# A hybrid decoder trunk on one core: three more warm-up matmuls, halved first loads on two queues, and other PSUM banks for the forget-gate turns

## The chip, the core and the metric

The kernel runs on one core of one Trainium2 chip. Everything is float32 data. The metric is the device time of the whole program in microseconds, the median of several executions; lower is better.

The engines are called as in the profile: PE is TensorE's matmul side and PEld its weight loads, DVE is VectorE, ACT is ScalarE, POOL is GpSimd, SP is SyncE. SP computes nothing here: it issues DMAs. ACT and POOL issue a few of them as well.

## The reference, cut to what matters

Two layers over a sequence of 256 tokens with 2048 features. Layer 0 mixes with two parallel recurrent groups, layer 1 with dilated attention; each layer ends in a squared-ReLU MLP with 8192 hidden features. What the change touches lies in layer 0, in its norm, its input projection and the HGRN2 group:

```python
hn = rms_norm(h, norm_mix[0])
proj = hn @ w_in                        # 2048 -> 6144 columns
x_lru, y_lru, q_h, f_h, v_h, g_h = split(proj)
# HGRN2, 8 heads of width 128, chunkwise
q = silu(q_h)
log_f = log(lower_bound + (1 - lower_bound) * sigmoid(f_h))
k = (1 - lower_bound) * sigmoid(-f_h)
# per chunk: decayed products of q and k, applied to v, and a carried state
...
h = h + concat(lru, hgrn) @ w_out
h = h + square(relu(rms_norm(h, norm_mlp[0]) @ w1)) @ w2
```

## The kernel before, in words

**Matmuls.** A float32 operand is held as two parts, `hi` (the value cast to a shorter float32 form) and `lo` (the rest). A product takes three matmuls, hi·hi, hi·lo and lo·hi; below, such a group is called a triple. ACT makes `hi` by a cast and DVE makes `lo` by a subtraction, for each weight tile of 128x2048 and for the activations (`bufa`, `bufb`). The matmuls are issued through `mm`, which chains each to the one before: PE's order is that of the code. All of them carry line 241 in the profile, and the turns (transposes on PE through the identity `ident`) line 244. All operations of DVE and ACT carry line 68, the helper that can keep an engine in written order. Outside that helper's ordered part, which begins after the first projection group, a scheduler with its own model of times decides the order on DVE, ACT and SP.

**The opening.** Line 301 issues WARM = 9 matmuls of 128x128 on a tile of ones; their result is not used. Each is two records in the profile (x18 for nine). Then `fetch_first` (line 206) loads the first inputs. The tensor `head` holds, for each of the first 8 slabs of 128 features, the tokens' values (256 columns) beside the first weight columns (512). Slabs 0 to 3 come as four pieces of 384 KB, slabs 4-5 and 6-7 as two of 768 KB (line 213), then `x_in` with the other slabs and the weight tiles `raw` (lines 221, 224). All are issued by SP; the small table `cols` (gains, biases) is issued by ACT (line 303). For each slab ACT scales the tokens (`bufa`, hi) and casts the weights (`hi`), and DVE makes the two lo parts. The first projection group, v0, is computed slab by slab (`by_k`): for each slab two triples, one for each half of the tokens, accumulated in two PSUM tiles `p`.

**Counters of DMAs.** Each DMA that SP or ACT issues reports its landing on one of eight counters, given out in turn in the order of the program. Before a counter is used again, the issuing engine waits until its last DMA has landed. So at most eight such DMAs are under way, and the ninth issue waits for the first landing.

**The groups of layer 0.** The projection is computed in groups of 512 columns in the order `v0 x0 x1 q0 G0 f0 q1 f1 G1 v1 g0 y0 g1 y1` (G0 and G1 are the gates of the LRU). Between halves of weight tiles, `tick` advances other work by one step, by the table TICKS. Lanes a and b each run `hgrn` for a pair of heads, hgrn(0) and hgrn(1) first, later hgrn(2) and hgrn(3). The first steps of one `hgrn`: turn q into a PSUM bank, take its sigmoid (ACT) and scale by it (DVE); turn f, take two sigmoids of it (ACT); then products of k and q in a bank of its own, and the levels c = 1, 2, 4 ... 128, each with matmuls into a tile named "pl". PSUM tiles: "pd" and "pt" have one bank each (lane a uses "pd", lane b "pt"), "pl" has two banks, which the LRU gates and the levels share, "p" has three, "po" one. A turn into a bank waits until the readers of its last contents are done.

Of the kernel before, what the change touches and what calls it, by code (L numbers as in the profile page):

```python
# [10 lines left out]
F32 = mybir.dt.float32  # L11
# [9 lines left out]
P = 128  # L21
S = 256
# [19 lines left out]
def trunk_kernel(ctx, tc, head, x, xtok, cols, tab, masks, pos, fin, w_in, w_gate, w_out, w_qkv, w_o, w1, w2, out):  # L42
    nc = tc.nc
# [9 lines left out]
    psc = pool("psc", 1, space=PSUM)  # L53
# [45 lines left out]
    both_in = opening.tile([P, 8, S + 512], F32, name="both_in")  # L99
# [32 lines left out]
    at = [0, 0]  # L132
# [73 lines left out]
    def fetch_first():  # L206
        for u in range(4):
            at[0] += 1
            if u < 2:
                made[u] = Weights(None, 0)  # L210
                m = u + 1
                for k in range(4 * u, 4 * u + 4, m):
                    nc.sync.dma_start(both_in[:, k:k + m], head[:, k:k + m])
                    for i in range(k, k + m):
                        split_to(bufa[:, i], both_in[:, i, :S], col("nmix0", i))
                        made[u].split((i - 4 * u) * 512, 512, both_in[:, i:i + 1, S:])
                continue
            r = wraw.tile([P, 2048], F32, name="raw")
            src, i = units[u]
            made[u] = Weights(r, 0)  # L220
            nc.sync.dma_start(x_in[:, 4 * u - 8:4 * u - 4], x[:, 4 * u - 8:4 * u - 4])
            n = 1024 if u == 2 else 2048
            for m in range(0, 2048, n):
                nc.sync.dma_start(r[:, m:m + n], src[i][:, m:m + n])
            for m in range(2):
                for k in range(4 * u + 2 * m, 4 * u + 2 * m + 2):
                    split_to(bufa[:, k], x_in[:, k - 8], col("nmix0", k))
                made[u].split(1024 * m, 1024)
# [14 lines left out]
    def turn(out_, in_):  # L243
        chain[:] = [after(T.transpose(out_, in_, ident), chain)]  # L244
# [26 lines left out]
    def lut(out_, in_, func, **kw):  # L271
        i = A.activation(out_, in_, func, **kw)
        if luts["kind"] != tables[func]:
            luts.update(kind=tables[func], before=luts["now"], now=[])
        luts["now"].append(after(i, luts["now"][:1] or luts["before"]))
# [8 lines left out]
    def split_to(dst, src, gain=None):  # L284
        if gain is None:
            h, l = dst[..., :S], dst[..., S:]
            A.copy(h, src)
            V.tensor_tensor(l, src, h.bitcast(F32), OP.subtract)
        else:
            A.activation(dst[:, :S], src, AF.Copy, scale=gain)  # L290
            V.scalar_tensor_tensor(dst[:, S:], src, gain, dst[:, :S].bitcast(F32),
                                   op0=OP.mult, op1=OP.subtract)
# [6 lines left out]
    warm = psc.tile([P, P], F32, name="po", bufs=1)  # L299
    for _ in range(WARM):  # L300
        T.matmul(warm, ones, ones, start=True, stop=True)
    with tc.high_priority():
        nc.scalar.dma_start(c_, cols)
        fetch_first()
# [92 lines left out]
    m = tmp.tile([P, 2], F32, name="nm2", bufs=2)  # L397
# [93 lines left out]
    done = {"v0": vfirst}  # L491
    outs, roots, rooms = {}, {}, {}

    def turned(name, tiles, at):
        p = psc.tile([P, 2, S], F32, name=name, bufs=1)
        for i, (z, m) in enumerate(zip(tiles, at)):
            for j in range(2):
                turn(p[:, i, j * P:j * P + P], z[:, j, m * P:m * P + P])
        return p
# [4 lines left out]
    def hgrn(c2):  # L504
        g, at = c2 // 2, 2 * (c2 % 2)
        bank = "pt" if at else "pd"
# [4 lines left out]
        f = xall[:, slot + 1024:slot + 1536].rearrange("p (h s) -> p h s", h=2)  # L511
        rest = [slot + 1536]
        p = turned(bank, [done[f"q{g}"]] * 2, (at, at + 1))
        lut(qp, p, AF.Sigmoid)
        for h, hd in enumerate(heads):
            V.scalar_tensor_tensor(qp[:, h], p[:, h], omlb[:, hd:hd + 1], qp[:, h], op0=OP.mult, op1=OP.mult)
        yield
        p = turned(bank, [done[f"f{g}"]] * 2, (at, at + 1))
        lut(f, p, AF.Sigmoid)
        lut(kq, p, AF.Sigmoid, scale=-1.0)  # L520
        for h, hd in enumerate(heads):
# [13 lines left out]
        while c <= 128:  # L535
            yield
            pl = psc.tile([P, 2, 2, 64], F32, name="pl", bufs=2)
# [60 lines left out]
    def finish(g, half):  # L598
        if not half:
            hs = roots[g]  # L600
            V.tensor_scalar(hs, hs, 1.0 / P, EPS, op0=OP.mult, op1=OP.add)
            roots[g] = wk.tile([P, 8], F32, name="hr", bufs=2)
            rsqrt(roots[g], hs, 8)
            yield
        pair_ = [2 * half, 2 * half + 1]
        for at in pair_:
            o, z = outs[4 * g + at], done[f"g{g}"][:, :, at * P:at * P + P]
            s = wk.tile([P, 2, P], F32, name="g", bufs=2)
            lut(s, z, AF.Sigmoid)
            V.tensor_tensor(s, s, z, OP.mult)  # L610
            for j in range(2):
                V.scalar_tensor_tensor(o[:, j], o[:, j], roots[g][:, 2 * at + j:2 * at + j + 1], s[:, j],
                                       op0=OP.mult, op1=OP.mult)
        yield
        p = turned("po", [outs[4 * g + at] for at in pair_], (0, 0))
        if g and not half:
            bufb.tiles[3] = act.tile([P, 4, 2 * S], F32R, name="bufb3")
        for i, at in enumerate(pair_):
            split_to(bufb[:, 8 + 4 * g + at], p[:, i], col("gn", 4 * g + at))
        yield  # L620
# [66 lines left out]
    def reload():  # L687
        for j in range(2):
            nc.sync.dma_start(xres[:, j], xtok[:, j])

    lanes.update(a=[hgrn(0), hgrn(2)], b=[hgrn(1), hgrn(3)],
                 c=[lru_in(0, 0), lru_in(0, 1), lru_in(1, 0), lru_in(1, 1),
                    lru_gelu(0), lru_out(0, 0), lru_out(0, 1), lru_gelu(1), lru_out(1, 0), lru_out(1, 1)],
# [421 lines left out]
    for g in range(4):  # L1115
        z = columns(8 + 8 * g, "qk", 2, True)
        todo = [steps.pop(0) if steps else [] for _ in range(14)]
        for i in range(4):
            turned, scores, weights, mixed = attend(4 * g + i, z)
# [18 lines left out]
    done = [n for n in range(4) if n != LAST]  # L1138
    rr = []
    with urgent():  # L1140
        for j in range(2):
            m = tmp.tile([P, 1], F32, name="fm", bufs=2)
# [15 lines left out]
        for j in range(2):  # L1158
            for n, e in ((0, A), (1, V), (3, A), (LAST, V)):
                at = slice(n * 512, n * 512 + 512)  # L1160
# [7 lines left out]
            for h in range(2):  # L1168
                at = slice(h * 1024, h * 1024 + 1024)
# [21 lines left out]
}  # L1191
PLACE = {step: n for n, step in enumerate(step for step in ORDER.split() if step[0] != "G")}
WARM = 9
ONES = 240
PLACES = ((2, 3, 5, 6), (2, 5, 8, 9), (3, 7, 10, 11), (4, 9, 12, 13))
LINE = 64
# [98 lines left out]
```

## Time and profile before

| | |
|---|---|
| median of 3 runs | 2128.49 us (2128.37, 2128.49, 2129.51) |
| the profiled execution | 2129.77 us, of which its span 2128.0 us |
| PE busy | 2116.4 us (99% of the span), 9822 matmul records |
| PEld, DVE, ACT busy | 1763.7, 1779.9, 1310.7 us |
| POOL busy | 72.3 us |
| HBM read, written | 496.41 MB, 2.10 MB (234 GB/s over the span) |

The profile is of one execution. Its times are counted from the start of the span. A row of the timeline has start, duration (both us), engine, line, operation, output <- inputs, count, and in brackets the idle time of the engine just before it and what ended that. The ends of matmuls are modelled, and neighbouring matmuls overlap. Queues are marked by a q: SPq is SP issuing a DMA, and a row there tells of the issue, not of the transfer.

### The profile page before, as it was taken

To read this page: it belongs to the slowest core of one execution; us is meant where nothing else is said; L and a number is where in the kernel's file an instruction comes from. 1 tells how busy PE (TensorE), PEld (TensorE's weight loads), DVE (VectorE), ACT (ScalarE), POOL (GpSimd) and SP (SyncE) were. 2 spreads that over 40 slices of the span, in tenths; PEclk is the share of its full clock that TensorE was granted. 3 is DMA by queue.
4 is the path that set the end of the run, shared out by engine and by line. 5 is a ranking of instruction groups with operands and counts; after the bars stand their busy time and mean duration, and the time that the engine had idled before them with its cause. 6 is when DMAs were issued, how large, how long until landed. Compare 5 with 4: busy or idle time off the path is not lost.

```text
span 2128.0 us, 24856 instructions
## 1 busy us (share of the span) xinstructions
PE 2116.4 (99%) x9822; PEld 1763.7 (83%) x9822; DVE 1779.9 (84%) x1687; ACT 1310.7 (62%) x1325; POOL 72.3 (3%) x89
## 2 busy tenths in 40 slices
PE   9999999999999999999999999999999999999998
PEld 8888888888888888888888888888888888888887
DVE  6666768988888888888998888798988987988897
ACT  7556466666566566566665666566755655755664
POOL 0000000000000000000000000000000000000000
PEclk9999999999999999999999999999999999999999
DMA  8543456787878778787778667567788778787874
GB/s 336 187 158 141 165 190 217 227 264 242 254 240 271 249 247 249 266 254 227 241 266 257 218 204 224 205 217 241 235 249 280 234 243 270 244 256 238 275 260 157
DMA packets 70164, 500.12 MB, mean 235 GB/s; under 512 B 7840, under 2 KB 8096, under 8 KB 10272
## 3 DMA queue, kind: packets, MB, share of 16 engines
q1 hardware_dynamic: 57888, 412.99, 50.7%
q0 software_dynamic: 11872, 84.94, 21.2%
q8 instruction: 77, 1.26, 0.2%
q10 hardware_dynamic: 288, 0.61, 0.1%
q14 instruction: 39, 0.32, 0.0%
HBM read 496.41 MB, written 2.10 MB: 234 GB/s over the span
## 4 chain that ended last, share of the span: by engine, by line
PE 96%; DVE 2%; ACT 1%; issue 0%; DMA 0%; DVEq 0%; ACTq 0%
PE p L241 60%; PE pd L241 15%; PE po L241 14%; PE pt L241 3%; PE pl L244 2%; PE pl L241 2%; DVE lo L68 1%; ACT hi L68 1%; ACT bufb L68 0%; ACT tk L68 0%; DVE xc L68 0%; DMA both_in<-in_head 0%; DVE tk L68 0%; DVE bufb L68 0%; DVE xall L68 0%
## 5 line engine op out<-in xcount | busy, mean ns | idle before, releaser
L68 DVE TENSOR_TENSOR lo<-raw,hi 128x2048 fp32r<-128x2048 f32 (+1 forms) x364 | 788.7, 2171 | 236.3 <-ACT hi L68 235.1
L68 ACT CAST hi<-raw 128x2048 fp32r<-128x2048 f32 (+1 forms) x364 | 659.3, 1817 | 497.6 <-PE p L241 306.8
L241 PE MATMUL p<-hi,bufa 128*128 128x512 f32 x2000 | 644.7, 393 | 0.6 <-ACT bufa L68 0.6
L241 PEld LDWEIGHTS p<-hi,bufa 128*128 128x128 f32 x2000 | 376.4, 188 | 78.3 <-ACT bufa L68 0.9
L241 PE MATMUL p<-hi,bufb 128*128 128x512 f32 x1264 | 404.9, 390 | 0.0
L241 PE MATMUL p<-lo,bufa 128*128 128x512 f32 x1000 | 389.9, 390 | 0.0
L68 DVE TENSOR_TENSOR lo<-s,hi 128x2048 fp32r<-128x2048 f32 x120 | 274.1, 2284 | 11.4 <-ACT hi L68 9.4
L241 PEld LDWEIGHTS p<-hi,bufb 128*128 128x128 f32 x1264 | 237.3, 188 | 49.0
L68 ACT CAST hi<-s 128x2048 fp32r<-128x2048 f32 x120 | 229.6, 1913 | 51.4 <-PE po L241 22.6
L241 PE MATMUL p<-lo,bufb 128*128 128x512 f32 x632 | 245.9, 389 | 0.0
L241 PEld LDWEIGHTS p<-lo,bufa 128*128 128x128 f32 x1000 | 188.4, 188 | 37.7
L241 PEld LDWEIGHTS p<-lo,bufb 128*128 128x128 f32 x632 | 118.7, 188 | 24.2
L241 PE MATMUL pd<-hi,bufa 128*128 128x512 f32 x352 | 116.7, 393 | 0.0
L241 PE MATMUL p<-hi,formx 128*128 128x512 f32 x352 | 116.2, 391 | 0.0
L68 DVE TENSOR_TENSOR lo<-t,hi 128x2048 fp32r<-128x2048 f32 x40 | 91.5, 2287 | 15.9 <-ACT hi L68 15.9
L241 PE MATMUL po<-hi,bufb 128*128 128x512 f32 (+1 forms) x320 | 102.3, 386 | 0.0
L241 PE MATMUL p<-hi,formh 128*128 128x512 f32 x288 | 94.5, 389 | 0.0
L68 DVE TENSOR_TENSOR s<-s,raw 128x2048 f32<-128x2048 f32 x40 | 91.2, 2281 | 0.6 <-DMA raw<-in_w_qkv 0.6
L68 DVE TENSOR_TENSOR s<-raw,t 128x2048 f32<-128x2048 f32 x40 | 91.3, 2283 | 0.2 <-DMA raw<-in_w_o 0.2
L68 ACT ACTIVATE y<-y 128x512 f32<-128x512 f32 x112 | 68.8, 630 | 28.1 <-DVE y L68 27.3
L241 PE MATMUL po<-hi,bufa 128*128 128x512 f32 x256 | 84.9, 393 | 0.0
L68 ACT CAST hi<-t 128x2048 fp32r<-128x2048 f32 x40 | 76.5, 1914 | 12.3 <-PE po L241 6.3
(293 smaller groups left out, 2786.9 us busy)
## 6 DMA issues: line engine op xcount, KB each, us to landing
raw<-in_w SPq DMA_DIRECT2D x224, 1024.0 KB, 6.5
raw<-in_w_in SPq DMA_DIRECT2D x45, 1024.0 KB, 4.8
raw<-in_w_qkv SPq DMA_DIRECT2D x42, 1024.0 KB, 6.5
t<-in_w SPq DMA_DIRECT2D x32, 1024.0 KB, 6.5
t<-in_w POOLq DMA_DIRECT2D x32, 1024.0 KB, 8.6
s<-in_w POOLq DMA_DIRECT2D x32, 1024.0 KB, 8.8
raw<-in_w_out SPq DMA_DIRECT2D x15, 1024.0 KB, 4.8
raw<-in_w_o SPq DMA_DIRECT2D x15, 1024.0 KB, 4.8
```

Of the source, the lines that this page charges most:

```text
L68: i = call(*args, **kw)
L241: chain[:] = [after(T.matmul(*args, **kw), chain)]
L244: chain[:] = [after(T.transpose(out_, in_, ident), chain)]
```

## The change

Three edits. WARM goes from 9 to 12. Each of the four pieces for slabs 0 to 3 is loaded as two DMAs of 64 partitions, the lower half issued by SP and the upper half by ACT; the pieces of slabs 4-5 and 6-7 stay whole and on SP. The turns of the forget gates f go into a "pl" bank (of which there are two) in place of the bank of the lane, "pd" or "pt", that holds q.

```diff
@@ fetch_first
                 for k in range(4 * u, 4 * u + 4, m):
-                    nc.sync.dma_start(both_in[:, k:k + m], head[:, k:k + m])
+                    for half, queue in enumerate((nc.sync, nc.sync if u else nc.scalar)[:1 if u else 2]):
+                        ps_ = slice(0, P) if u else slice(64 * half, 64 * half + 64)
+                        queue.dma_start(both_in[ps_, k:k + m], head[ps_, k:k + m])
                     for i in range(k, k + m):
@@ turned
-        p = psc.tile([P, 2, S], F32, name=name, bufs=1)
+        p = psc.tile([P, 2, S], F32, name=name, bufs=2 if name == "pl" else 1)
@@ hgrn
-        p = turned(bank, [done[f"f{g}"]] * 2, (at, at + 1))
+        p = turned("pl", [done[f"f{g}"]] * 2, (at, at + 1))
         lut(f, p, AF.Sigmoid)
@@
-WARM = 9
+WARM = 12
```

## The prediction

> **What bounds the kernel now.** I read the page first, for the share of TensorE.
>
> ```profile
> span 2128.0 us, 24856 instructions
> ## 1 busy us (share of the span) xinstructions
> PE 2116.4 (99%) x9822; PEld 1763.7 (83%) x9822; DVE 1779.9 (84%) x1687; ACT 1310.7 (62%) x1325; POOL 72.3 (3%) x89
> ```
>
> PE is busy for 2116.4 of 2128.0 us, so only 11.6 us can be saved by taking waits away. Next I asked for the list of waits on PE alone, over the whole span.
>
> ```profile
> PE pd L244 <- DVE xall L68: 1.4, 1, 1.4
> PE po L301 <- DVE e L68: 1.1, 1, 1.1
> PE p L241 <- ACT bufa L68: 0.6, 1, 0.6
> PE pt L244 <- DVE xall L68: 0.2, 1, 0.2
> ```
>
> Columns: total us, times, longest. Four waits, 3.3 us in all: the start (1.1), the gap between warm-up and first real matmul (0.6), and one pair of turns that waits for its banks (1.4 and 0.2). The busy time of each engine by stretch says whether anything else gives way.
>
> ```profile
> 20.00:100.00 80.00, 80.00 (x375) 66.80 (x374) 56.18 (x112) 49.01 (x51) 0.70 (x1) 1.00 0.66 246
> 132.00:320.00 188.00, 188.00 (x1016) 161.89 (x1015) 124.82 (x200) 102.51 (x172) 0.00 (x0) 1.00 0.45 164
> 320.00:2119.00 1799.00, 1798.81 (x8207) 1493.54 (x8207) 1560.13 (x1312) 1115.81 (x1032) 71.36 (x84) 1.00 0.76 242
> ```
>
> The second and third columns are the stretch and PE's busy time: the same number, but for 0.2 us. So whatever PE gains or loses before 20 us, or around 129 us, arrives at the end undiminished, and nothing else pays. The other 11.6 - 3.3 = 8.3 us lie behind the last matmul and are not touched.
>
> The order in which the changed program was built agrees with this reading: PE's sequence is the old one with three warm-up matmuls more and other bank names at the eight forget-gate turns of each group. On VectorE and ScalarE it differs in the first 15 us, in some small operations after v0, and by a few neighbours swapped near 350 us. PE was not idle in either place (rows above), so these go at nothing, with PE's own matmuls as their cover; without it each would cost one small operation, under 1 us. So there are two terms.
>
> **Term 1, the forget gates.** In `hgrn` the f turn now takes a "pl" bank, where it took the bank that the q turn of the same lane had filled.
>
> ```profile
> 125.31 0.69 ACT L68 ACTIVATE tk<-p,nr 128x512 f32<-128x512 f32 x1 [0.33 <-PE p L241]
> ```
> ```profile
> 129.17 0.86 DVE L68 SCALAR_TENSOR_TENSOR xall<-pt,omlb,xall 128x256 f32<-128x256 f32 x2
> ```
> ```profile
> 129.39 0.63 PE L244 MATMUL pd<-tab__183,tk 128*128 128x128 f32 x4 [1.40 <-DVE xall L68]
> 130.18 0.63 PE L244 MATMUL pt<-tab__183,tk 128*128 128x128 f32 x4 [0.16 <-DVE xall L68]
> ```
>
> PE stood 1.40 and then 0.16 us until VectorE had read q out of "pd" and "pt" (the second read is the middle row). The data of f0 were there from about 126.0 (125.31 + 0.69, upper row). Is a "pl" bank free then? Here are its last reader before and its next writer after:
>
> ```profile
> 102.83 0.87 ACT L68 ACTIVATE bufb<-pl,c__91 128x256 f32<-128x256 f32 x2
> ```
> ```profile
> 143.37 1.89 PE L241 MATMUL pl<-xall 128*128 128x64 f32 x16
> ```
>
> It ended at 103.7, 24 us earlier; the next user of "pl", the first level, is the second row, 14 us later. So 1.56 us go, once: the same turns of the second group, near 219 us, have no entry in the list of waits. What is late next? After the turn PE goes on with the second half of a weight tile whose first half it has just used, so nothing new is awaited. Term 1: **-1.56 us**, between 0 and -1.6.
>
> **Term 2, the opening.** Here is who starts what before.
>
> ```profile
> 0.74 3.07 SPq L213 DMA_DIRECT2D both_in<-in_head  x6
> 0.74 0.40 ACTq L303 DMA_DIRECT2D c__91<-in_cols  x1
> ...
> 1.05 4.21 PE L301 MATMUL po<-nr 128*128 128x128 f32 x18 [1.05 <-DVE e L68]
> ...
> 4.98 0.88 SPq L224 DMA_DIRECT2D raw<-in_w_in  x2
> ...
> 5.90 0.79 PE L241 MATMUL p<-hi,bufa 128*128 128x512 f32 x1 [0.63 <-ACT bufa L68]
> ...
> 10.31 0.33 SPq L396 DMA_DIRECT2D xall<-in_xtok  x1
> 10.31 0.51 ACT L68 ACTIVATE bufa<-both_in,c__91 128x256 fp32r<-128x256 f32 x1 [0.81 <-DMA both_in<-in_head]
> ```
>
> Nine warm-ups take 4.21 us, so twelve take 5.61 and end at 6.66: 0.76 us after the first real matmul started before. By itself that is a loss. It is paid back if the matmul rate doubles sooner:
>
> ```profile
> 5.90:9.47 3.57, 3.57 (x8) 2.83 (x9) 3.24 (x7) 2.91 (x6) 0.00 (x0) 1.00 1.00 358
> 9.47:13.40 3.93, 3.93 (x18) 3.25 (x17) 3.25 (x8) 3.12 (x8) 0.00 (x0) 1.00 1.02 420
> ```
>
> Eight matmuls in 3.57 us (0.45 each), then eighteen in 3.93 (0.22 each): the slow rate cost 8 x 0.23 = 1.8 us here, although the column of the granted clock says 1.00 in both. That is the most a better warm-up could bring.
>
> But I think neither sets the start any more; the order of the loads does. Eight counters serve the DMAs of SP and ACT in turn, and a ninth DMA waits until the holder of its counter has landed. Before, six pieces and x_in were issued without such a wait, and the ninth DMA (row 4.98) waited for `cols`. With eight halves in place of four pieces, the piece of slabs 4 and 5 is now the ninth: SP holds it until `cols` has landed, at 4.98 instead of about 2.8 (the fifth of six in 3.07 us from 0.74). Behind it on SP stand piece 6-7, x_in and the first weight tiles, each held by the counter of a half that is early; POOL's queue is not passed. And the second half of slab 3 stands on ACT's queue behind slab 1's casts. The scheduler has accordingly put slabs 4 and 5 **ahead of slab 3** on ACT and DVE, while PE still takes slab 3 first. So PE now waits for three slabs' work that begins when piece 4-5 lands (call that T).
>
> T: bytes moved in the stretches of before,
>
> ```profile
> 0.00:4.98 4.98, 3.93 (x18) 3.92 (x18) 0.19 (x3) 1.65 (x3) 0.20 (x4) 1.00 0.64 190
> 4.98:6.97 1.99, 1.36 (x5) 0.91 (x4) 1.50 (x4) 1.82 (x4) 0.00 (x0) 1.00 0.96 324
> 6.97:8.48 1.51, 1.51 (x5) 1.22 (x4) 1.48 (x3) 1.02 (x2) 0.00 (x0) 1.00 1.01 372
> 8.48:10.31 1.83, 1.83 (x7) 1.41 (x7) 1.42 (x3) 1.01 (x2) 0.00 (x0) 1.00 1.01 420
> ```
>
> (last column GB/s) are 946, 645, 562 and 769 KB, 2922 in all when piece 4-5 landed at 10.3. The late half of slab 3 (197 KB) now comes behind it, which is worth 0.47 us at 420 GB/s: T = 9.8. The lower end is the issue at 4.98 plus the fastest landing of such a piece,
>
> ```profile
> DMA to landing us min/median/max: 4.1/5.8/8.8
> ```
>
> 4.98 + 4.1 = 9.1; the upper end is the old 10.3. I take 9.7, near the row of bytes. Three slabs from there, as before from the row 10.31:
>
> ```profile
> 12.04 0.39 PE L241 MATMUL p<-lo,bufa 128*128 128x512 f32 x1
> ...
> 13.37 0.68 DVE L68 TENSOR_TENSOR lo<-both_in,hi 128x512 fp32r<-128x512 f32 x1
> 13.40 0.39 PE L241 MATMUL p<-lo,bufa 128*128 128x512 f32 x1
> ```
>
> The third slab's lo part ended at 13.37 + 0.68 = 14.05, that is 3.74 us after its piece landed. So slab 3's lo is ready at 9.7 + 3.74 = 13.45, and PE's matmul on it (row 12.04 before) starts 1.4 to 1.5 us later. Bounds: +0.8 (T = 9.1) to +2.1 (T = 10.3). Slabs 0 to 2 fit ahead of it at either rate: 18 matmuls from 6.66, the first 6 or so slow, end by about 12. The longer warm-up therefore costs nothing and brings nothing; without that cover it would cost 0.76 or bring up to 1.8. Later slabs come with more slack than before, as PE is later and their loads aren't. Four more issues on ACT (0.40 each, the `cols` row) lie in time in which ACT waited for data. Term 2: **+1.5 us**.
>
> [...]
>
> **The sum.** -1.56 + 1.5 = -0.1 us, with bounds -0.7 to +0.5. The profiled execution took 2129.77 us (span 2128.0 and 1.8 around it), so it gives 2129.7. The runs shown are 2128.37, 2128.49 and 2129.51; the profile lies with the highest. Two clusters 1.1 us apart are about what the slow rate is worth at the start (1.8 at most), so I read them as executions in which the rate rose earlier and later. After the change the wait for slab 3 swallows either, so I set out from the upper cluster: 2129.5 - 0.1, a little less for the case that the gap is only the profiler's: **2129.3 us**. That is 0.04% above the median; about 0.2% (4.3 us) is what a measurement of this kernel can tell from no change.
>
> [...]
>
> **Rivals.**
> (a) The halves help: from two queues the first pieces and `cols` land about 1 us sooner, piece 4-5 is issued at 4 and lands near 8.3, and slab 3 is no later than before. It decides where T is under 8.5. For: only 190 GB/s moved in the first 4.98 us. Against: that is the DMAs' own start, with SP issuing faster than they drained. The sum is then -1.5: 2128.0. Chance 0.2.
> (b) The second half of slab 3, issued behind slab 1's casts at about 7, lands last of all: after about 12, when ACT reaches slab 3. With the 4.1 us of the fastest landing it comes at 11.1, with the median 5.8 at 12.8, then some 0.9 us more: 2130.2. Chance 0.1.
> (c) Slower: PE stands idle ahead of slab 3 for some 2 us, and the matmul rate falls back. Then it runs another 3.6 us at 0.45 us a matmul, 1.8 us lost: 2131.1. It decides where the idle time is long enough to count. Against: the gap of 1.40 us before 129.39 left the rate as it was. Chance 0.07. [...]
> (d) The turn doesn't gain: f still waits, in "pl" or for its own data, and 1.56 us stay: 2130.9. Chance 0.03.
> My forecast has the other 0.6; its own range is 2127.8 to 2130.1.
>
> **How the numbers follow.** The range takes in (a) from the lower cluster, 2128.4 - 1.5 = 2126.9, and (c) at 2131.1: 2127.0 to 2131.2. For a change over 4.3 us two of the losses would have to meet at their upper ends, or something outside this list: 0.02 slower, 0.01 faster, 0.97 within 0.2%.
>
> **What would show it.** In the profile after: no PE wait on "xall" near 128 us; SP's issue of piece 4-5 near 5 us; ACT taking slabs 4 and 5 ahead of 3; a PE wait of 1 to 3 us ahead of the seventh triple of matmuls (slab 3), with slab 3's lo matmul at 13.0 to 14.1 against 12.04. I am wrong if slab 3 starts by 12.1, if the f turns still wait, or if PE idles anywhere after 20 us.

## The result, and the profile after

The changed kernel takes 2132.99 us (median of 15 runs, 2131.58 to 2133.88) where the kernel before, run beside it, took 2128.49 (15 runs, 2127.90 to 2129.60): a ratio of 1.0020, 95% interval 1.0013 to 1.0027. It is slower by 4.5 us, 0.21%, just beyond the bound of 0.2%, which the prediction had given a chance of 0.02, and outside its range. The profiled execution took 2133.84 us, its span 2132.1.

The page of the kernel after, and under it its list of waits on PE (total us, times, longest):

```profile
span 2132.1 us, 24878 instructions
...
PE 2118.6 (99%) x9828; PEld 1764.1 (83%) x9828; DVE 1781.0 (84%) x1687; ACT 1310.0 (61%) x1325; POOL 72.3 (3%) x89
```
```profile
PE p L243 <- ACT hi L68: 4.0, 3, 2.9
PE po L303 <- DVE e L68: 1.1, 1, 1.1
PE p L243 <- DVE lo L68: 0.4, 2, 0.2
```

The two waits on "xall" are gone, and 4.4 us of waits ahead of 16 us stand in their place (0.6 before), one of them 2.9 us long. PE itself is busy 2.2 us longer, of which the longer warm-up makes 0.08 (4.29 us, below, against 4.21). Both show in the timeline of PE after: the first warm-up, the first product, the last of slab 2, the first four of slab 3, then the turns.

```profile
1.05 4.29 PE L303 MATMUL po<-nr 128*128 128x128 f32 x24 [1.05 <-DVE e L68]
6.13 0.51 PE L243 MATMUL p<-hi,bufa 128*128 128x512 f32 x1 [0.78 <-ACT hi L68]
...
11.98 0.39 PE L243 MATMUL p<-hi,bufa 128*128 128x512 f32 x1
15.22 0.79 PE L243 MATMUL p<-hi,bufa 128*128 128x512 f32 x1 [2.86 <-ACT hi L68]
15.95 0.79 PE L243 MATMUL p<-lo,bufa 128*128 128x512 f32 x1
16.54 1.05 PE L243 MATMUL p<-hi,bufa 128*128 128x512 f32 x2
...
127.91 0.60 PE L246 MATMUL pd<-tab__190,tk 128*128 128x128 f32 x4
134.24 1.03 PE L246 MATMUL pl<-tab__190,tk 128*128 128x128 f32 x8
140.57 1.05 PE L243 MATMUL pd<-xall 128*128 128x128 f32 x8
```

Slab 3's lo matmul starts at 15.95, against 12.04 before: 3.9 us late. The windows after say what follows (stretch, PE busy and matmuls, then the other engines, granted clock, DMA share, GB/s):

```profile
12.37:15.22 2.85, 0.00 (x0) 0.00 (x0) 1.79 (x5) 1.55 (x4) 0.00 (x0) 0.81 1.03 342
15.22:20.80 5.58, 5.58 (x12) 4.09 (x13) 5.46 (x11) 5.58 (x11) 0.00 (x0) 0.50 1.04 393
```

The same stretch before:

```profile
15.22:20.80 5.58, 5.58 (x26) 4.64 (x25) 5.36 (x10) 5.08 (x10) 0.00 (x0) 1.00 1.03 432
```

After 2.85 us without a matmul, PE ran 12 matmuls in 5.58 us where it had run 26, with a granted clock of 0.50. The q turn and the k-q product before stood here:

```profile
121.51 0.60 PE L244 MATMUL pd<-tab__183,tk 128*128 128x128 f32 x4
...
136.13 1.05 PE L241 MATMUL pd<-xall 128*128 128x128 f32 x8
```

So the q turn comes at 127.91 against 121.51, 6.4 us late: 3.9 of it from the late slab, and what is left, 2.5, from the fallen rate. From there to the k-q product it takes 12.66 us against 14.62 before, 1.96 less. The difference, 4.4, is still there at the output's DMA (issued at 2122.22 against 2117.86); the two spans differ by 4.1.

Why slab 3 is late shows on ACT's timeline after; the row at 7.60 is the issue of the second half of slab 3.

```profile
7.55 0.51 ACT L68 ACTIVATE bufa<-both_in,c__91 128x256 fp32r<-128x256 f32 x1 [1.48 <-DMA both_in<-in_head]
7.60 0.50 ACTq L215 DMA_DIRECT2D both_in<-in_head  x1
...
9.15 0.51 ACT L68 ACTIVATE bufa<-both_in,c__91 128x256 fp32r<-128x256 f32 x1 [0.57 <-DMA both_in<-in_head]
...
10.92 0.51 ACT L68 ACTIVATE bufa<-both_in,c__91 128x256 fp32r<-128x256 f32 x1 [0.75 <-DMA both_in<-in_head]
...
14.15 0.51 ACT L68 ACTIVATE bufa<-both_in,c__91 128x256 fp32r<-128x256 f32 x1 [1.30 <-DMA both_in<-in_head]
```

Slabs 1, 2 and the piece 4-5 land at 7.55, 9.15 and 10.92. The half issued at 7.60, after slab 1 had landed, comes last of all, at 14.15. And the DMAs were slower while they were busy all the time, in the window from 2 to 8 us, after and then before:

```profile
2.00:8.00 6.00, 5.00 (x28) 4.21 (x26) 1.18 (x2) 2.95 (x6) 0.00 (x0) 1.00 1.04 262
```
```profile
2.00:8.00 6.00, 5.37 (x21) 4.71 (x20) 2.53 (x5) 3.67 (x8) 0.00 (x0) 1.00 0.94 319
```

262 GB/s against 319, though the DMA engines' share is 1.04 against 0.94.

### The profile page after: what moved, and what is told of

Same layout as the page of the kernel before. It is cut to its first block, busy times and chain, and to the rows that moved or that the text cites. A ratio compares the mean times of both kernels' runs of the same rounds, so it can differ in the third digit from the quotient of the medians.

```text
span 2132.1 us, 24878 instructions
## 1 busy us (share of the span) xinstructions
PE 2118.6 (99%) x9828; PEld 1764.1 (83%) x9828; DVE 1781.0 (84%) x1687; ACT 1310.0 (61%) x1325; POOL 72.3 (3%) x89
## 4 chain that ended last, share of the span: by engine, by line
PE 97%; DVE 1%; ACT 1%; DMA 1%; issue 0%; ACTq 0%
PE p L243 61%; PE pd L243 15%; PE po L243 14%; PE pt L243 3%; PE pl L246 2%; PE pl L243 2%; DMA both_in<-in_head 1%; ACT hi L68 0%; DVE lo L68 0%; ACT tk L68 0%; DVE tk L68 0%; PE po L246 0%; DVE ho L68 0%; PE pd L246 0%; DVE g L68 0%
```

## The experiments

Three more sets of runs, each with the kernel before on the same chip; its medians there were 2129.01, 2128.95 and 2128.38 us (31 runs each), beside the 2128.49 of the result. Differences below are to the one of the same set.

**Each edit alone.** First the f turns alone.

```diff
-        p = psc.tile([P, 2, S], F32, name=name, bufs=1)
+        p = psc.tile([P, 2, S], F32, name=name, bufs=2 if name == "pl" else 1)
-        p = turned(bank, [done[f"f{g}"]] * 2, (at, at + 1))
+        p = turned("pl", [done[f"f{g}"]] * 2, (at, at + 1))
```

> Of the change only the bank edit: the forget-gate turns in pl, nine warm-ups, whole pieces. If PE's two waits of 1.56 us before 129 us go and nothing takes their place, the median is 1.6 to 2.0 us under that of before, near 2126.7 (the stretch from the q turn to the first k-q product, 14.6 us before, becomes 12.7). If the gain is taken back by a later wait, it stays at 2128.5.

2127.20 us, 1.8 below before; ratio 0.9991 (0.9982 to 1.0000). The runs still lie in two groups, 2125.7 to 2126.5 and 2127.2 to 2127.8. From its timeline:

```profile
120.58 0.60 PE L244 MATMUL pd<-tab__183,tk 128*128 128x128 f32 x4
126.91 1.03 PE L244 MATMUL pl<-tab__183,tk 128*128 128x128 f32 x8
133.24 1.05 PE L241 MATMUL pd<-xall 128*128 128x128 f32 x8
```

The same 12.66 us from the q turn to the k-q product as in the kernel after: this edit gains 1.96 us in both.

The warm-up alone:

```diff
-WARM = 9
+WARM = 12
```

> Of the change only the twelve warm-ups. The runs of before lie in two groups, 2127.9 to 2128.6 and 2129.3 to 2129.6. If the groups are executions in which the matmul rate rose within the warm-ups and after them, twelve warm-ups put nearly all into the lower group: median 2128.2 to 2128.5, no run over 2129. If the longer warm-up only delays the first real matmul, 0.8 us slower: 2129.3. If it shortens the slow stretch for the median too, 1 us or more faster: under 2127.5.

2128.58 us (2127.79 to 2129.18), 0.4 below before; ratio 0.9997 (0.9989 to 1.0006): no difference of the medians that can be told. The expectation had no run over 2129; two of the eleven are, where the kernel before had 17 of 31 in this set.

The halves alone:

```diff
-                    nc.sync.dma_start(both_in[:, k:k + m], head[:, k:k + m])
+                    for half, queue in enumerate((nc.sync, nc.sync if u else nc.scalar)[:1 if u else 2]):
+                        ps_ = slice(0, P) if u else slice(64 * half, 64 * half + 64)
+                        queue.dma_start(both_in[ps_, k:k + m], head[ps_, k:k + m])
```

> Of the change only the halves. If the late second half of slab 3 and the fall of the matmul rate in the wait for it make the whole loss, slab 3 starts after 14.5 us, the next 5 us run at 0.43 us a matmul, and the median is 6 us over that of before, 2133.5 to 2135.5. If the loss needs the longer warm-up as well (PE early and then idle), it is 3 to 4 us: 2132. If the halves are harmless, 2128.5.

2134.56 us (2132.37 to 2135.93), 5.6 above; ratio 1.0025 (1.0015 to 1.0034). The whole loss is this edit's.

The change without the halves (the first two diffs together):

> The change without the halves: twelve warm-ups and the pl banks, whole pieces. If the halves alone lose, this is faster than both kernels: 2126.3 to 2126.9, the bank edit's gain with the upper group of runs gone. If the longer warm-up costs its 0.8 us, 2127.5.

2126.39 us (2125.72 to 2126.68, 11 runs), 2.6 below; ratio 0.9988 (0.9979 to 0.9996): faster than both kernels. Its list of waits on PE:

```profile
PE po L301 <- DVE e L68: 1.1, 1, 1.1
PE p L241 <- ACT bufa L68: 0.2, 1, 0.2
```

All its runs lie within 1.0 us, and the upper group is gone: none of eleven, where the f turns alone had six of eleven. So twelve warm-ups do something: 0.8 us of median against the f turns alone. The changed kernel is 7.1 us worse than this one, to its own set's before (+4.5 and -2.6). The other runs divide these 7.1 us.

**Second set: issue, order, rate, queue.** The upper halves issued by ACT before its first table load:

```diff
+        for k in range(4):
+            nc.sync.dma_start(both_in[:64, k:k + 1], head[:64, k:k + 1])
+            uppers = [after(nc.scalar.dma_start(both_in[64:, k:k + 1], head[64:, k:k + 1]), uppers)]
+        after(lut_spare(), uppers)
```

> The changed kernel with all four upper halves issued by ACT at its start, ahead of the load of its function table; ACT and DVE still take slabs 4 and 5 ahead of slab 3. If the late issue of the last half (7.60 us) makes the wait, that half lands by about 9, slab 3 then waits only for the work on slabs 4 and 5 (lo part at 10.9 + 3.7 = 14.7 us in place of 15.9), PE's idle time falls under 2 us and the matmul rate stays up: 2129 to 2130.5, some 3 us faster than the changed kernel. If the order of the slabs makes it, it stays within 1 us of 2133.

2132.98 us, 4.0 above; ratio 1.0017 (1.0008 to 1.0027). The expectation missed: issuing earlier was not enough. From PE's timeline:

```profile
14.65 0.49 PE L247 MATMUL p<-hi,bufa 128*128 128x512 f32 x1 [2.48 <-ACT hi L68]
...
16.57 0.86 PE L247 MATMUL p<-hi,bufa 128*128 128x512 f32 x2
```

ACT had issued all four halves by 4.54, but it still took slabs 4 and 5 first, and their piece had landed by 11.74: slab 3 waited behind them, PE idled 2.48 us, and from 16.57 the matmuls slowed (0.86 us for a pair that takes 0.62). The halves issued by ACT took 6.1 us to land, in the median. The last was expected by about 9; with the same early issue and the slabs in order (below), ACT could take slab 3 at 11.69.

Twelve unused matmuls in the wait ahead of slab 3, so that PE doesn't idle:

```diff
+                if by_k and src is w_in and (g, i, j) == (0, 3, 0):
+                    idle = psc.tile([P, P], F32, name="pt", bufs=1)
+                    for _ in range(FILL):
+                        mm(idle, ones, ones, start=True, stop=True)
```

> The changed kernel with twelve unused matmuls (as the warm-ups) put into PE's wait ahead of slab 3. If the idle time of 2.9 us there lets the matmul rate fall, it now stays up, slab 3 starts as late as before (15.2 us), and 2 to 3 us come back: 2130 to 2131. If the rate falls for another reason, or if slabs 4 to 8 then wait for their loads, it stays near 2133.

2130.81 us, 1.9 above; ratio 1.0008 (0.9998 to 1.0017). PE's timeline:

```profile
11.87 2.84 PE L243 MATMUL pt<-nr 128*128 128x128 f32 x24
14.79 0.50 PE L243 MATMUL p<-hi,bufa 128*128 128x512 f32 x1
...
16.54 0.62 PE L243 MATMUL p<-hi,bufa 128*128 128x512 f32 x2
```

Slab 3 comes hardly earlier (14.79 against 15.22), but the pair at 16.54 takes 0.62 us, where in the kernel after the pair at 16.54 (one triple behind in the work) took 1.05. More work made the kernel faster: 2.6 us (+4.5 against +1.9), of which 0.43 is that slab 3 came sooner; the rest, 2.2, is what the fallen rate costs.

All halves on SP:

```diff
-                    for half, queue in enumerate((nc.sync, nc.sync if u else nc.scalar)[:1 if u else 2]):
+                    for half, queue in enumerate((nc.sync, nc.sync)[:1 if u else 2]):
```

> The changed kernel with both halves on SP's queue: halves, and one DMA more than there are counters, but nothing on ACT's queue; the slabs are then in order on ACT and DVE. If the second queue makes the loss, this is within 1.5 us of the kernel with whole pieces, 2126.4 to 2128. If halves land slower as such (64 partitions each), the first slabs stay late (slab 1 at 7.5, slab 2 at 9.1 us), and it loses 2 us or more: over 2128.5.

2128.20 us (2127.50 to 2129.51), 0.7 below; ratio 0.9997 (0.9987 to 1.0006). Its window:

```profile
2.00:8.00 6.00, 5.49 (x29) 4.76 (x27) 2.13 (x4) 2.67 (x6) 0.00 (x0) 1.00 1.00 253
```

253 GB/s with one queue: the second queue isn't what makes the halves slow. The time lies between the two ranges expected (up to 2128, and over 2128.5). But on one queue the slabs land in the order of their use, slab 3 at 10.63, and PE waits often and shortly (0.35 us at the most) in place of once and long.

The changed kernel with slabs 0 to 5 in order on ACT and DVE:

```diff
+                InOrder.on = True
                 ...
+                InOrder.on = False
```

> The changed kernel with ACT and DVE held to the slabs' order, 3 ahead of 4 and 5; the last half is issued as late as before. If the order of the slabs made slab 3 late, its lo matmul comes back to 12 to 13 us and the time to 2128 to 2129.5. If the landing of its late half (14.15 us) sets it, nothing is won there and slabs 4 and 5 come later than in the changed kernel: 2133 to 2135.

2132.55 us, 3.6 above; ratio 1.0015 (1.0005 to 1.0024). ACT's timeline:

```profile
14.43 0.51 ACT L68 ACTIVATE bufa<-both_in,c__91 128x256 fp32r<-128x256 f32 x1 [4.71 <-DMA both_in<-in_head]
```

Slab 3 is now next in line, and ACT waits 4.71 us for it: with the late issue it is the landing that binds, not the order. The time is just under the range expected for that (2133 to 2135).

**Third set: what makes the halves slow.** Early issue and slabs in order, both:

```diff
+        after(lut_spare(), uppers)
                 ...
+                InOrder.on = True
```

> The changed kernel, with the four upper halves issued by ACT ahead of its first table load (as in the run with the uppers first), and with the slabs taken in the order 0 to 5 on ACT and DVE while they are cast. Neither a late landing nor the slab order is left. Theory (halves move at some 255 GB/s from whatever queue, late issue and order do the rest): DMA at 250 to 290 GB/s from 2 to 8 us, slab 3 starts on PE at 12 to 13 after waits of under 1.5 us each, no return to the slow matmul rate, 2127.5 to 2129. Rival (two queues at the same time are themselves the loss): slab 3 not before 14, an idle time of over 2 us, 2131.5 to 2133.5.

2129.36 us (2128.66 to 2130.34), 1.0 above; ratio 1.0005 (0.9996 to 1.0014). PE's timeline:

```profile
12.76 0.49 PE L249 MATMUL p<-hi,bufa 128*128 128x512 f32 x1 [0.95 <-ACT hi L68]
```

Slab 3 starts at 12.76 and the rate doesn't fall (from 13.82 on a pair takes 0.62 to 0.64 us), as the theory said, with 270 GB/s from 2 to 8 us; the time is 0.4 us above the range expected. Removing the late issue and the order together brings 3.5 us, where each alone brought under 1.

Halves of even and odd partitions, all else as in the changed kernel:

```diff
-                        ps_ = slice(0, P) if u else slice(64 * half, 64 * half + 64)
+                        ps_ = slice(0, P) if u else slice(half, P, 2)
```

> The changed kernel, with each half made of the even or of the odd partitions instead of the lower or upper 64: the same eight DMAs of the same size, the same rows, the same queues, the same order on the engines. Theory A (a side of 64 neighbouring partitions takes its data slower): the DMAs move 350 GB/s or more from 2 to 8 us, slabs 1 and 2 land by 6.5 and 7.5 against 7.55 and 9.15; the last half of slab 3 is still issued near 7 and lands at 12 to 13; 2128 to 2131. Theory B (it is the number of DMAs, or 64 partitions in one, whichever they are): 250 to 280 GB/s, landings as before, 2132 to 2134.

2130.97 us (2129.34 to 2132.15), 2.6 above; ratio 1.0011 (1.0002 to 1.0020). The window, then two rows of ACT's timeline:

```profile
2.00:8.00 6.00, 5.77 (x29) 4.72 (x27) 2.15 (x4) 3.52 (x6) 0.00 (x0) 1.00 0.99 315
```
```profile
8.05 0.51 ACT L68 ACTIVATE bufa<-both_in,c__91 128x256 fp32r<-128x256 f32 x1 [0.57 <-DMA both_in<-in_head]
...
12.72 0.51 ACT L68 ACTIVATE bufa<-both_in,c__91 128x256 fp32r<-128x256 f32 x1 [0.57 <-DMA both_in<-in_head]
```

Same sizes, same queues, same order of issues, and 315 GB/s in place of 262, the rate of the kernel before (319); below the 350 expected, which was set too high by the best windows of before. Slab 2 lands 1.1 us sooner (8.05 against 9.15), slab 3 1.4 (12.72 against 14.15, its last half issued at 6.50 in place of 7.60). So it is which 64 partitions stand in a DMA, not how many. The edit also changes which rows of the source stand in it, and no run tells the two apart. What is left is the late issue: PE idles 2.51 us for slab 3, and the rate falls (granted clock 0.73 from 15.22 to 20.80 us).

Halves of the columns, 128 partitions each:

```diff
+                        cs_ = slice(0, S + 512) if u else slice(384 * half, 384 * half + 384)
+                        queue.dma_start(both_in[:, k:k + m, cs_], head[:, k:k + m, cs_])
```

> The changed kernel, with each of the four pieces split by columns (all 128 partitions, 384 of the 768 columns in each DMA), on the same two queues. Here ACT issues its third and fourth half ahead of slab 2's casts and the slabs go in order. Theory A (64 partitions are what is slow): 350 GB/s or more from 2 to 8 us, slab 3 on PE by 12, no wait of over 1.5 us, 2126 to 2128. Theory B (the number of DMAs, or their smaller size, is what is slow): 250 to 290 GB/s, slab 3 on PE at 12.5 to 14.5, 2128 to 2132.

2131.92 us (2130.21 to 2133.98), 3.5 above; ratio 1.0016 (1.0006 to 1.0025). The window, then ACT:

```profile
2.00:8.00 6.00, 5.91 (x27) 5.35 (x26) 2.45 (x5) 4.23 (x8) 0.00 (x0) 1.00 1.00 347
```
```profile
4.92 0.35 ACTq L215 DMA_DIRECT2D both_in<-in_head  x1
...
5.34 0.42 ACTq L215 DMA_DIRECT2D both_in<-in_head  x1
...
12.04 0.62 ACT L68 CAST hi<-both_in 128x512 fp32r<-128x512 f32 x1 [4.13 <-DMA both_in<-in_head]
```

The rate is near that of theory A (347 for 350 or more), the time that of theory B. Both are explained by the rows: ACT's third and fourth half were issued at 4.92 and 5.34, behind slab 0's scaling, and by 5.24 SP had issued its four halves and both pieces of 768 KB. Slab 2's weights came at 12.04, 7.1 us after their issue, PE idled 2.87 us and the rate fell (0.70 from 12.37 to 15.22). The normal DMA rate didn't help a transfer that was issued late.

Whole pieces from two queues:

```diff
+                    (nc.scalar if k in (1, 3) else nc.sync).dma_start(both_in[:, k:k + m], head[:, k:k + m])
```

> The changed kernel with whole pieces again, those of slabs 0 and 2 issued by SP and those of slabs 1 and 3 by ACT. Tells the second queue apart from the halves. Theory (the halves are slow, not the second queue): 350 GB/s or more from 2 to 8 us, slabs 0 to 2 landed by 7.5, 2126 to 2128.5 if slab 3 is not held by ACT's order, up to 2130.5 if it is. Rival (transfers from two queues slow each other): under 300 GB/s, 2130 to 2133.

2128.83 us (2128.29 to 2129.00), 0.5 above; ratio 1.0002 (0.9992 to 1.0011). Its window, and that of the kernel without halves, all on SP:

```profile
2.00:8.00 6.00, 6.00 (x28) 5.35 (x26) 2.42 (x5) 3.96 (x8) 0.00 (x0) 1.00 0.97 366
```
```profile
2.00:8.00 6.00, 5.75 (x30) 5.02 (x29) 2.56 (x6) 3.64 (x8) 0.00 (x0) 1.00 0.93 327
```

Two queues did not slow each other here: 366 against 327 GB/s. The six pieces were all issued by 2.55 us, where SP alone took until 3.81. Still it is slower than the kernel without halves (+0.5 against -2.6). Here ACT took slab 2 before slab 1, and slabs 4 and 5 before 3, and PE waited for lo parts (0.31 and 0.39 us); that is a part of the 3.1 us, and the rest was not followed up.

## Why the prediction was wrong

**The 7.1 us, divided.** Whole pieces to halves on one queue: +1.9 (-2.6 to -0.7). From one queue to two, with the last half issued at 7.60: +2.6 (-0.7 to +1.9, the run with the filler). The idle time filled or not, which is mostly the rate: +2.6 (+1.9 to +4.5). The second is a difference of two sets of landings, not one removed wait.

**What bounds it** was right: what PE lost at the start arrived at the end (6.4 - 1.96 = 4.4 against 4.36 at the output's DMA).

**Term 1** was right in mechanism and too small: 1.96 for 1.56. From the q turn to the f turn the time fell by 1.55 (7.88 to 6.33), and another 0.41 behind it (0.16 of it the second listed wait): the turns now run as one row of 8 in 1.03 us, where two rows of 4 began 0.79 us apart. The list counts a wait from the modelled end of the matmul before it (0.39 us after its start), but in an unbroken row the next one starts after 0.23. So the wait removed here was worth more than its entry.

**Term 2** was put at +1.5 us, +2.1 at most; it measured +6.4 at the q turn. It failed at three steps. First, the count by bytes: the landings were taken from the byte curve of whole pieces, which no run had shown to hold for halves, and lower and upper halves moved 262 GB/s in place of 319. The piece 4-5 landed at 10.92, not 9.7. Second, the issue of the piece 4-5 near 4.98. The DMA views after and before have the time from the issue of `cols` to its landing:

```profile
c__91<-in_cols ACTq DMA_DIRECT2D x1, 80.0 KB, 1.9
```
```profile
c__91<-in_cols ACTq DMA_DIRECT2D x1, 80.0 KB, 4.2
```

It landed near 2.6, before SP came to its fifth issue, so the counter held nothing there:

```profile
3.31 0.59 SPq L215 DMA_DIRECT2D both_in<-in_head  x1
```

The piece 4-5 was issued at 3.31, sooner than forecast, and landed later all the same. Third, and the largest: the order of landings. I let slab 3's lo part be ready when slabs 4 and 5 had been worked on, at 13.45; the second half of slab 3 itself landed only after that, at 14.15. The prediction had that half behind the piece 4-5 in its count of bytes, and yet did not let slab 3 wait for it. That is rival (b), to which I gave 0.1 and at most 12.8, a median landing of 5.8 us after an issue near 7; it was 6.55 after 7.60.

**Rival (c)**, the fall of the rate, came true, at 0.07 and 1.8 us; it measured some 2.2. I had set (b) and (c) side by side as if only one could be. They are one chain: the later slab 3 lands, the longer PE idles, and with enough idle time the rate goes too. Their sum would have been about 2132, and this chain is what happened (2133.0). What spoke against it was the gap of 1.40 us, after which the rate had stayed; idle times of 2.86, 2.51 and 2.48 us were followed by the slow rate.

**The baseline.** The two clusters as an earlier and a later rise of the rate fit: with twelve warm-ups and no halves the upper one is gone. The profiled execution of the f turns alone, of the lower group (2126.21), has its nine warm-ups in 3.73 us, where that of the kernel before, of the upper group (2129.77), took 4.21:

```profile
1.06 3.73 PE L301 MATMUL po<-nr 128*128 128x128 f32 x18 [1.06 <-DVE e L68]
```

So in the first the rate had risen within the warm-ups. For the same reason twelve took 4.29 us in the kernel after, and not 5.61 as the prediction scaled them. In the eleven profiles with twelve warm-ups these took between 4.29 and 5.49 us; the three with nine have 3.73, 4.21 and 4.21. The first rise in the record of the granted clock stands at 3.91 us in the kernel after and at 9.59 in the kernel before.

**What would have shown it** did: the list had no "xall", ACT took 4 and 5 first, and a PE wait stood ahead of slab 3, but with its lo matmul at 15.95, outside 13.0 to 14.1.

## What to carry to other kernels

Splitting these loads in two did not make them land sooner: the bytes ahead of the last half decided. So ask when each half is issued, what stands ahead of that issue on its queue, and how many bytes are then already under way. When a forecast has a late transfer and an idle TensorE as two rivals, price them as one chain: in the kernel after, the idle time of 2.86 us cost about 2.2 us more in slow matmuls. Try the parts of a bundled change singly; here two of the three gave 2.6 us and the third took 7.1.

## What the runs showed of the hardware

- With the first four pieces as halves of partitions 0 to 63 and 64 to 127, the DMAs moved 253 to 270 GB/s from 2 to 8 us, from one queue or from two; even and odd partitions 315, halves of the columns 347, whole pieces 318 to 343 from one queue and 366 from two. The two runs that change nothing but which elements make up a half (315 and 347) put it on the choice of partitions, or of the source rows that go with them.
- An idle time of PE of 1.40 us (before, at 129.39) and of 1.27 us (early issue and order) left the matmul rate as it was; 2.48 us and more, in six kernels, were each followed by a slow stretch.
- Yet the length of one wait is not what decided. In the record of the granted clock of the kernel after, the clock rises at 3.91, falls at 14.15 and rises again at 20.97: 10.24 and 6.83 us apart, which is 3 and 2 times 3.413. The stretch behind them, 2106.02 us, is 617 times that, and the one of the kernel before, 2112.85 from 9.59 on, 619 times. So in these two profiles the changes of the clock lie on steps of 3.413 us. In the kernel after it fell at 14.15, 1.78 us into the wait; with the early issue the first slow row is the one at 16.57, 1.92 us behind its end.
- With the steps counted from those changes, what told falls apart was PE's idle time within one step. The clock fell behind a step with 1.78 us (the kernel after, from 10.74). It stayed up behind steps with 1.00 (the kernel after, from 3.91) and 1.06 (before, from 125.64). It rose behind steps with 0.56 us or less, and not behind 0.63 (before, from 2.76). In the kernel after, the slow step from 14.15 still held 1.07 us of idle time, and a second slow one followed; in the other five the clock was slow for some 3.4 us, an estimate from the granted clock of their windows (0.69 from 15.22 to 20.80 in three of them). For two, the halves of even and odd partitions and those of the columns, the windows place the fall near 14.84 and 13.48, behind some 2.6 and 2.9 us of idle time within 3.413: an estimate as well. The ends of matmuls are modelled, so these limits are only as good as that.
- The record begins with the first rise, 9.59 in the kernel before. So the granted clock of 1.00 that its windows show for the slow matmuls from 5.90 on is no measurement.
